# Early bias table, a reordered first step and a last tile stored as token rows in a one-core decoder layer

## The chip, the cores and the metric

The kernel runs on one core of one Trainium2 chip. The metric is the device time of one execution in microseconds (us). The engines are TensorE (PE in the profile, with PEld for its weight loads), VectorE (DVE), ScalarE (ACT), GpSimd (POOL) and SyncE (SP); each takes its instructions in the order in which the program lists them. SP, ACT and POOL also issue DMA transfers, which 16 DMA engines carry out; transfers issued by SP and ACT are the profile's hardware queues q1 and q10, those issued by POOL are its software queue q0.

## The reference

One step of a one-layer decoder with 1024 channels: 16 meta tokens and 2048 prompt tokens, and 8 sample tokens with caches. Cut to what matters here:

```python
def rmsnorm(x, g):
    return x * lax.rsqrt(jnp.mean(x * x, -1, keepdims=True) + 1e-6) * g

p = rmsnorm(x, norm1_g) @ w_in                  # 1024 -> 1792: q, k, v, GLU a, GLU b
u = p_a * sigmoid(p_b)
s = q @ k.T / 8 + rel_bias[t5_bucket(dist)]     # window 128, 8 heads, learned sinks
ao = softmax_with_sinks(s) @ v
cc = silu(layernorm(depthwise_conv31(u)))
x = x + concat(ao, cc) @ w_out                  # 1024 -> 1024
x = x + square(relu(rmsnorm(x, norm2_g) @ w_up)) @ w_down   # 1024 -> 4096 -> 1024
y = rmsnorm(x, norm_f_g)
```

The outputs are y for the prompt and for the samples, and the new key, value and convolution states. The change touches how the table `rel_bias[t5_bucket(dist)]` is laid out on the chip, the first matrix products, and how the last y leaves.

## The kernel before, in words

Channels lie on the partitions and tokens along the free dimension. The tokens are cut into five tiles of 384, 448, 448, 448 and 320 tokens; tile 0 carries the 16 meta tokens as well (400 columns), the last one the 8 samples (328 columns).

The weights come as 86 slabs of 128 x 1024 floats, used 424 times. One *step* (`pe_step`) multiplies one slab with one tile. Products keep fp32 accuracy by splitting each operand into two fp32r halves: the slab is loaded (`dma_slab`, SP, 512 KB), ACT casts it to `whi`, DVE subtracts for `wlo` (`split_slab`), and 24 products go into one PSUM buffer: for each of 8 chunks whi with the high and the low half of the activations, and then the 8 products with wlo. There are two `raw` buffers and three of each split half, so the load of slab k+2 waits for the `wlo` of slab k. PSUM: three buffers "mm" for steps, two "s" and two "pt" for attention (the fourth and fifth step of tile 0 borrow "pt"), one "st" for sums.

Slabs are counted here from 0, in the order in which they are loaded. The start is `norm1_first`: slab 0, the 8 chunks of tile 0, the split of h1 = x*g, and warm-up products. It does not wait for the row scale `rs` of the first norm; the step results are multiplied by `rs` when they leave PSUM (`ev0`). So the first result can leave only after `rs`, which takes 8 squares, sums on PE, a root, a reciprocal, a broadcast on PE and a copy on ACT (`rstd` with quick). Eight steps of tile 0 run like this, then tile 1 joins.

`bias_setup` builds the bias table for attention. A product on PE gives 8 heads x 384 values, ACT copies them to SBUF, POOL writes them to two tables in DRAM, `scr` (8 copies) and `skw` (16 copies, each a position further along), and 8 reads of `skw` (16 partitions each) fill `bias` with 128 x 8 x 256 values. Its reads wait until `skw` has landed. It is called ahead of the second step (nin == BAT). POOL also loads x of tile 1, ahead of it.

The end is `final_gen` for the last tile: squares on ACT, their sum over chunks on DVE, column sums on PE, root, reciprocal and broadcast, then 8 times y*g*rs on DVE, each stored as 128 x 328 by SP or ACT.

The Tile framework orders the instructions of each engine by a simulated time line and by priorities; a changed call place can therefore move others.

Of the kernel before, what the change touches and what calls it, by code (L numbers as in the profile page):

```python
# [7 lines left out]
F32 = mybir.dt.float32  # L8
F32R = mybir.dt.float32r
AF = mybir.ActivationFunctionType  # L10
ALU = mybir.AluOpType
PSUM = bass.MemoryType.PSUM

D = 1024
# [62 lines left out]
            self.step(DRAIN)  # L77


def trunk(tc, x_in, w_all, smalls, rel, ck, cv, sconv, y_out, kv_out, ck_out, cv_out, up_out, us_out):  # L80
    nc = tc.nc
    with ExitStack() as ctx:
        cp = ctx.enter_context(tc.tile_pool(name="cp", bufs=1))
# [130 lines left out]
        def pe_step(hi, lo, n, evac, budget, late=False, parts=1, keep=False, spare=False):  # L214
            k = cur[0]
            if not keep:
                cur[0] += 1
            while pos["split"] <= min(k + LA, len(order) - 1):
                split_slab()
            while pos["dma"] < min(k + LA + 1 + NRAW, len(order)):  # L220
                dma_slab()
            if late:
                flush()
            wh, wl = split[k] if keep else split.pop(k)
            if spare:
                ps = pa.tile([128, 512], F32, tag="pt", name="mm")
            else:
                ps = pm.tile([128, 512], F32, tag="mm", name="mm")
            o = ps[:, :n]
            seq = []  # L230
            if late:
                for c in range(8):
                    seq += [(wh, hi, c), (wh, lo, c), (wl, hi, c)]
            else:
                for c in range(8):
                    seq += [(wh, hi, c), (wh, lo, c)]
                seq += [(wl, hi, c) for c in range(8)]
            cut = [len(seq) * (p + 1) // parts for p in range(parts)]
            for j, (w, a, c) in enumerate(seq):
                mm(o, w[:, c, :], a[c], j == 0, j == len(seq) - 1)  # L240
                if j + 1 == cut[0]:
                    old = list(pend)
                    pend.clear()
                    for e in old:
                        e()
                if j + 1 in cut:
                    bg.step(budget / parts)
            pend.append(lambda: evac(ps))
# [116 lines left out]
        def norm1_first():  # L365
            s = st[0]
            n = TI[0]
            dma_slab()
            x = s["x"] = load_x(0)
            dma_slab()  # L370
            with tc.high_priority(2000):
                split_slab()
                warm = misc()
                for _ in range(WARM):
                    mm(warm[:, :128], ones, ones, True, True)
                s["h1h"], s["h1l"] = [], []
                for c in range(8):
                    hi = slot(F32R)
                    lo = slot(F32R)
                    act(hi[:, :n], x[c][:, :n], AF.Copy, scale=sm[:, G1 + c:G1 + c + 1])  # L380
                    stt(lo[:, :n], x[c][:, :n], sm[:, G1 + c:G1 + c + 1], f(hi[:, :n]), ALU.mult, ALU.subtract)
                    s["h1h"].append(hi)
                    s["h1l"].append(lo)
            split_slab()
            g1 = norm1_gen(1)
            next(g1)
            box = []
            s["rs"] = slot()
            for _ in ahead(run_stats(norm_stats(x, n, quick="a0" in QUICK, gate=s["h1h"][7], out=s["rs"]), box), 2000):
                pass  # L390
            return g1

# [515 lines left out]
        def down_step(i, g, d, budget):  # L908
# [10 lines left out]
                flush()  # L919
            pe_step([t[:, :n] for t in s["hh"]], [t[:, :n] for t in s["hl"]], n, ev, budget, late=d == 0)  # L920

        def final_gen(i):
            s = st[i]
            n = RT[i]
            s.setdefault("ydone", 0)
            box = []
            yield from run_stats(norm_stats(s["x2"], n, ready=lambda c: s["ydone"] > c,
                                             quick="f%d" % i in QUICK), box)
            rs = box[0]
            for c in range(8):  # L930
                y = s["x2"][c]
                stt(y[:, :n], y[:, :n], sm[:, GF + c:GF + c + 1], rs[:, :n], ALU.mult, ALU.mult)
                q = (nc.sync, nc.scalar)[c % 2] if i == NT - 1 else nc.gpsimd
                q.dma_start(y_out[:, YO[i] + c * n:YO[i] + (c + 1) * n], y[:, :n])  # L934
                yield

        def bias_setup():
            ps = misc()
            mm(ps[:NH, :EW], relt[:33, 0:NH], relt[:33, 8:8 + EW], True, True)
            e = slot()  # L940
            cpy(e[:NH, :EW], ps[:NH, :EW])
            nc.gpsimd.dma_start(scr.rearrange("p h x -> h p x"),
                                e[:NH, :EW].unsqueeze(1).broadcast_to([NH, NSMP, EW]))
            a = skw[:]
            row = NH * SKWW
            nc.gpsimd.dma_start(bass.AP(tensor=a.tensor, offset=a.offset, ap=[[SKWW, NH], [row + 1, NSKW], [1, EW]]),
                                e[:NH, :EW].unsqueeze(1).broadcast_to([NH, NSKW, EW]))
            for q in range(0, 128, NSKW):
                nc.gpsimd.dma_start(bias[q:q + NSKW], bass.AP(tensor=a.tensor, offset=a.offset + 127 - q,
                                                              ap=[[row, NSKW], [SKWW, NH], [1, 256]]))  # L950
# [80 lines left out]
        for op in prog:  # L1031
            k = op[0]
            if k == "in":
                _, i, m = op
                if i == 0:
                    if nin == N1AT:
                        gens["n1"] = [bg.add(g1)]
                    if nin == BAT:
                        bias_setup()
                    nin += 1  # L1040
                win_step(i, m, 24 * (TI[i] / 2400.0) - 1.2 - 0.6, spare=i == 0 and nin in (4, 5))
            elif k == "in2":
                m = op[1]
                win_step(0, m, 24 * (TI[0] / 2400.0) - 1.2 - 0.6, keep=True)
                win_step(1, m, 24 * (TI[1] / 2400.0) - 0.6)
            elif k == "conv0":
                flush()
                gens["conv"] = [bg.add(ahead(conv_gen(0), HP0, lambda: "ln" in st[0])), bg.add(conv_pe_gen(0), True)]
            elif k == "attn0":
                flush()  # L1050
                gens["attn"] = [bg.add(attn_gen(0, range(j, PT[0] // BQ[0], NS0)), A0F) for j in reversed(range(NS0))]
            elif k == "out":
                _, i, m = op
                wout_step(i, m, ff_budget(i, False))
            elif k == "ff":
                _, i, t, g, c = op
                b = ff_budget(i, t == "u")
                if t == "u":
                    up_step(i, g * 8 + c, b)
                else:  # L1060
                    down_step(i, g, c, b)
            elif k == "bg":
                i = op[1]
                flush()
                cat_alloc(i)
                gens["attn"] = [bg.add(attn_gen(i, range(j, PT[i] // BQ[i], NS1))) for j in range(NS1)]
                if i == NT - 1:
                    gens["attn"].append(bg.add(sample_gen(i)))
                gens["conv"] = [bg.add(ahead(conv_gen(i), HPC, lambda: "ln" in st[i]))]
            elif k == "sync_bg":  # L1070
                flush()
                bg.drain(gens["attn"] + gens["conv"])
            elif k == "n1":
                gens["n1"] = [bg.add(norm1_gen(op[1]))]
            elif k == "sync_n1":
                bg.drain(gens["n1"])
            elif k == "n2":
                gens["n2"] = [bg.add(ahead(norm2_gen(op[1]), HPN if op[1] else HPN0))]
            elif k == "sync_n2":
                flush()  # L1080
                bg.drain(gens["n2"])
            elif k == "fin":
                gens["fin"] = [bg.add(ahead(final_gen(op[1]), HPF if op[1] == NT - 1 else 0))]
                if op[1] == NT - 1:
                    flush()
                    bg.drain()
# [14 lines left out]
HPC = 0  # L1101
HPN = 0
HPN0 = 300
HPF = 0
COV = 5
BAT = 1
WARM = 12
N1AT = 3
A0F = True
QUICK = ["a0", "a1", "l0", "m0", "b0", "f4"]  # L1110
NS0 = 2
NS1 = 1
NPB = 2
# [6 lines left out]
def _pack(inp):  # L1120
# [62 lines left out]


_OUTS = [
    ("y_out", (128, 8 * sum(RT))), ("kv_out", (128, 2, 128 + NSMP)), ("ck_out", (128, 1024)),
    ("cv_out", (128, 1024)), ("up_out", (128, 4, CW - 1)), ("us_out", (128, 4, NSMP, CW)),
]

# [38 lines left out]
```

## Time and profile before

| | us |
|---|---|
| median of 3 runs | 2097.62 (2097.12 to 2098.48) |
| profiled execution, whole time | 2097.54 |
| its span, first to last instruction | 2095.7 |
| PE busy in the span | 2068.3 (99%) |
| DVE busy | 1525.2 (73%) |
| ACT busy | 1181.0 (56%) |
| mean granted TensorE clock | 0.993 of full |

The span is followed by 1.8 us that the profile does not show. A busy share is a mean over the whole span; the start (about 75 us) and the end (about 12 us) have other limits than the middle, and they are read from stretches of their own.

### The profile page before, as it was taken

What the parts mean: (1) busy time and instruction counts of PE and PEld (TensorE: products, weight loads), DVE (VectorE), ACT (ScalarE), POOL (GpSimd) and SP (SyncE); (2) the same over time, 40 slices, a digit from 0 to 9 for tenths busy, and PEclk for the clock granted to TensorE, in tenths of its full rate; (3) what the DMA queues carried; (4) which work ended last, traced back from release to release, by engine and by line L of the source; (5) the groups of instructions that cost most, each with busy time, mean ns of one, the idle gap of its engine ahead of it and who ended that gap; (6) DMA issues with size and microseconds to landing.
All of it is one profiled execution on the core that took longest, in us unless ns stands there. A gap on an engine that the chain in (4) does not pass through costs nothing.

```text
span 2095.7 us, 30054 instructions
## 1 busy us (share of the span) xinstructions
PE 2068.3 (99%) x11354; PEld 1961.5 (94%) x11354; DVE 1525.2 (73%) x2603; ACT 1181.0 (56%) x2154; POOL 55.8 (3%) x111
## 2 busy tenths in 40 slices
PE   9899999999999999999999999999999999999998
PEld 8688899999999999999999999999999999999997
DVE  7896798977858987658669886567797754564444
ACT  7577565667456456564454647555646465454443
POOL 3000000000000000000000000000011000000000
PEclk9899999999999999999999999999999999999999
DMA  7113233334532222234323222244433322444443
GB/s 209 47 37 111 100 122 104 128 114 160 179 111 101 101 101 101 101 136 162 129 104 108 101 101 101 101 172 150 142 117 112 123 105 101 151 162 151 151 143 105
DMA packets 77536, 254.39 MB, mean 121 GB/s; under 512 B 9661, under 2 KB 20037, under 8 KB 77392
## 3 DMA queue, kind: packets, MB, share of 16 engines
q1 hardware_dynamic: 72000, 238.08, 32.5%
q0 software_dynamic: 4672, 13.65, 2.3%
q8 instruction: 89, 1.46, 0.3%
q10 hardware_dynamic: 720, 0.76, 0.1%
q14 instruction: 55, 0.45, 0.1%
HBM read 241.97 MB, written 10.47 MB: 120 GB/s over the span
## 4 chain that ended last, share of the span: by engine, by line
PE 95%; DVE 2%; DMA 1%; ACT 1%; issue 0%; POOL 0%; SPq 0%; DVEq 0%; ACTq 0%; POOLq 0%
PE mm L159 89%; PE st L159 2%; PE pt L595 1%; PE s L159 1%; DVE t L119 1%; DMA bias<-skw 0%; DMA skw<-t 0%; DVE t L115 0%; PE cps L159 0%; DVE m L119 0%; ACT p L135 0%; DMA raw<-w_all 0%; DVE p L576 0%; DMA sm<-smalls 0%; ACT L134 0%
## 5 line engine op out<-in xcount | busy, mean ns | idle before, releaser
L159 PE MATMUL mm<-t,whi 128*128 128x448 f32 (+3 forms) x6560 | 1330.9, 349 | 3.1 <-ACT t L138 0.8
L159 PEld LDWEIGHTS mm<-t,whi 128*128 128x128 f32 x6560 | 1164.1, 188 | 58.2 <-DVE t L115 2.9
L138 ACT CAST whi<-raw 128x1024 fp32r<-128x1024 f32 x424 | 443.5, 1049 | 546.6 <-PE mm L159 430.2
L159 PE MATMUL mm<-t,wlo 128*128 128x448 f32 (+3 forms) x3280 | 702.6, 347 | 0.0
L115 DVE TENSOR_TENSOR wlo<-raw,whi 128x1024 fp32r<-128x1024 f32 x424 | 516.6, 1218 | 224.7 <-PE mm L159 123.5
L159 PEld LDWEIGHTS mm<-t,wlo 128*128 128x128 f32 x3280 | 587.9, 188 | 24.9
L119 DVE SCALAR_TENSOR_TENSOR t<-u,sm,t 128x448 f32<-128x448 f32 (+1 forms) x480 | 300.5, 645 | 3.5
L115 DVE TENSOR_TENSOR t<-mm,t 128x448 f32<-128x448 f32 (+2 forms) x200 | 116.5, 583 | 184.5 <-PE mm L159 181.4
L115 DVE TENSOR_TENSOR t<-m,t 128x448 fp32r<-128x448 f32 (+3 forms) x236 | 134.1, 581 | 25.8 <-ACT t L138 25.1
L138 ACT CAST t<-m 128x448 fp32r<-128x448 f32 (+3 forms) x236 | 125.3, 536 | 18.8 <-DVE m L119 14.6
L134 ACT ACTIVATE m<-mm 128x448 f32<-128x448 f32 (+2 forms) x176 | 90.2, 512 | 51.0 <-PE mm L159 49.5
L134 ACT ACTIVATE m<-t 128x448 f32<-128x448 f32 (+3 forms) x140 | 71.7, 542 | 61.7 <-DVE t L115 43.0
L134 ACT ACTIVATE m<-m 128x448 f32<-128x448 f32 (+3 forms) x164 | 90.1, 549 | 4.5 <-DVE m L115 0.6
L135 ACT ACTIVATE p<-p,nm 112x240 f32<-112x240 f32 (+3 forms) x152 | 72.3, 477 | 27.3 <-DVE nm L124 25.9
L576 DVE CUSTOM_DVE_ANT_0 p<-s,bias,sm 112x240 f32<-112x240 f32 (+3 forms) x152 | 61.1, 449 | 6.2 <-DMA bias<-skw 3.8
L134 ACT ACTIVATE p<-p,rd 112x240 f32<-112x240 f32 (+3 forms) x152 | 61.9, 476 | 3.9 <-DVE rd L130 3.5
L115 DVE TENSOR_TENSOR ss<-ss,m 128x448 f32<-128x448 f32 (+3 forms) x100 | 58.4, 584 | 6.3 <-ACT m L134 2.8
L934 POOL DMA_DIRECT2D y_out<-t x32 | 17.3, 543 | 1602.6 <-DVE t L119 1601.4
L130 DVE RECIPROCAL rs<-m 128x448 f32<-128x448 f32 (+2 forms) x15 | 41.6, 2776 | 23.9 <-ACT m L134 23.9
L119 DVE SCALAR_TENSOR_TENSOR t<-t,sm 128x384 f32<-128x384 f32 (+1 forms) x98 | 58.3, 612 | 0.9
L159 PE MATMUL mm<-cal,whi 128*128 128x448 f32 (+2 forms) x160 | 55.3, 347 | 0.2 <-DVE cal L115 0.2
L159 PE MATMUL mm<-cah,whi 128*128 128x448 f32 (+2 forms) x160 | 55.3, 347 | 0.0
(178 smaller groups left out, 1159.6 us busy)
## 6 DMA issues: line engine op xcount, KB each, us to landing
raw<-w_all SPq DMA_DIRECT2D x424, 512.0 KB, 3.2
t<-x_in SPq DMA_DIRECT2D x40, 224.0 KB, 4.6
y_out<-t POOLq DMA_DIRECT2D x24, 224.0 KB, 3.3
t<-x_in SPq DMA_DIRECT2D x16, 164.0 KB, 3.5
t<-x_in POOLq DMA_DIRECT2D x8, 224.0 KB, 4.3
t<-x_in SPq DMA_DIRECT2D x8, 200.0 KB, 4.6
t<-x_in SPq DMA_DIRECT2D x8, 192.0 KB, 3.8
y_out<-t POOLq DMA_DIRECT2D x8, 192.0 KB, 4.7
```

The source lines that it names most:

```text
L115: return nc.vector.tensor_tensor(out, a, b, op=op)
L119: return nc.vector.scalar_tensor_tensor(out, a, s, b, op0=op0, op1=op1)
L130: return nc.vector.reciprocal(out, a)
L134: return nc.scalar.activation(out, a, f, bias=bias, scale=scale)
L135: return nc.scalar.activation(out, a, f, bias=bias, scale=scale, accum_out=accum_out)
L138: return nc.scalar.copy(out, a)
L159: return nc.tensor.matmul(out, lhsT, rhs, start=start, stop=stop)
L576: nc.vector.tensor_tensor_reduce(out=p[:bq, c, :nk], in0=sp[c // 2][:bq, c % 2, :nk], in1=bias[:bq, h, b0:b0 + nk], scale=1.0, scalar=sm[: ...
L595: nc.tensor.transpose(t[:r, c * bq:(c + 1) * bq], p[:bq, c, a:a + r], idn[:bq, :bq])
L934: q.dma_start(y_out[:, YO[i] + c * n:YO[i] + (c + 1) * n], y[:, :n])
```

## The change

Three things are changed.

1. In the first step (`k == 0`) the 24 products are interleaved: chunk c with whi, then the two products of chunk c-1 that need `wlo` or the low half.
2. `bias_setup` is called in `norm1_first`, with a PSUM buffer of its own ("s"), and its POOL part is tied by a one-column copy to the eighth `h1h`. The gate of the squares moves from `h1h[7]` to `h1l[7]`.
3. The last tile ends in `final_last`: y*g is formed in place chunk by chunk, without rs. PE turns it (24 transposes, three windows of 110 tokens by 8 chunks of 128 channels) into six PSUM banks of 110 x 512; the sums of squares are taken per token, so that the scale is one value per partition; ACT and DVE scale the six banks into SBUF, and six stores of 109 or 110 rows x 512 floats (2 KB a row) go to a new output `yl_out`. The host no longer turns the last tile.

```diff
+            if k == 0:
+                for c in range(9):
+                    if c < 8:
+                        seq += [(wh, hi, c)]
+                    if c > 0:
+                        seq += [(wl, hi, c - 1), (wh, lo, c - 1)]
...
+                bias_setup(s["h1h"][7])
...
-            for _ in ahead(run_stats(norm_stats(x, n, quick="a0" in QUICK, gate=s["h1h"][7], out=s["rs"]), box), 2000):
+            for _ in ahead(run_stats(norm_stats(x, n, quick="a0" in QUICK, gate=s["h1l"][7], out=s["rs"]), box), 2000):
...
+        def final_last(i):
...
+            w = -(-n // 3)
+            at0 = [0, w - 1, n - w]
+            rows = [w - 1, n - 2 * w + 1, w]
...
+                if c == 7:
+                    yg.append(tmp())
+                    ts(yg[c][:, :n], y[:, :n], g, None, ALU.mult)
+                else:
+                    act(y[:, :n], y[:, :n], AF.Copy, scale=g)
...
+                for b in range(3):
+                    o = slice(at0[b], at0[b] + w)
+                    mm(ps[:w, b:b + 1], ssum[:, o], ones[:, 0:1], True, False)
+                    mm(ps[:w, b:b + 1], sqs[7][:, o], ones[:, 0:1], False, True)
+                act(r[:w, :3], ps[:w, :3], AF.Sqrt, bias=epst[:w], scale=1.0 / D)
+                recip(r[:w, :3], r[:w, :3])
+            for b in range(3):
+                nc.vector.tensor_copy(tb[b][1][:1, :1], sqs[7][:1, :1])
...
+                    if k % 2 == 0:
+                        act(o, tb[b][h][:w], AF.Copy, scale=r[:w, b:b + 1])
+                    else:
+                        ts(o, tb[b][h][:w], r[:w, b:b + 1], None, ALU.mult)
+                    q = nc.scalar if k == 4 else nc.sync
+                    q.dma_start(yl_out[at0[b]:at0[b] + rows[b], h * 512:h * 512 + 512], o[:rows[b]])
...
-                q = (nc.sync, nc.scalar)[c % 2] if i == NT - 1 else nc.gpsimd
-                q.dma_start(y_out[:, YO[i] + c * n:YO[i] + (c + 1) * n], y[:, :n])
+                nc.gpsimd.dma_start(y_out[:, YO[i] + c * n:YO[i] + (c + 1) * n], y[:, :n])
...
-        def bias_setup():
-            ps = misc()
+        def bias_setup(gate):
+            ps = pa.tile([128, 512], F32, tag="s", name="bs")
...
+            nc.gpsimd.tensor_copy(e[:NH, :1], f(gate[:NH, :1]))
...
-                    if nin == BAT:
-                        bias_setup()
...
-QUICK = ["a0", "a1", "l0", "m0", "b0", "f4"]
+QUICK = ["a0", "a1", "l0", "m0", "b0"]
```

What the order of the instructions makes of it is shown at three places.

POOL near the start, before: the loads of tile 1 (x_in), then the two tables, then the reads into the bias table. What a row waits for stands in brackets (DMASW: a POOL transfer, Activation: ACT).

```order
L355 DMA t<-x_in 128x448 [waits DMASW3_49,Pool_49]
L355 DMA t<-x_in 128x448 [waits DMASW4_49,Pool_49]
L942 DMA scr<-t 8x8x384 [waits DMASW5_49,Activation_49]
L946 DMA skw<-t 8x16x384 [waits DMASW6_49]
L634 DMA sbias<-scr 64x129 [waits DMASW7_49,DMASW5_49]
L949 DMA bias<-skw 16x8x256 [waits DMASW6_49,DMASW0_49]
```

The same place now:

```order
L361 DMA t<-x_in 128x448 [waits Pool_49]
L1017 DMA scr<-t 8x8x384 [waits Activation_49]
L1021 DMA skw<-t 8x16x384 [waits DMASW3_49]
L361 DMA t<-x_in 128x448 [waits DMASW4_49,Pool_49]
L361 DMA t<-x_in 128x448 [waits DMASW5_49,Pool_49]
L361 DMA t<-x_in 128x448 [waits DMASW6_49,Pool_49]
L641 DMA sbias<-scr 64x129 [waits DMASW7_49,DMASW2_49]
L1024 DMA bias<-skw 16x8x256 [waits DMASW3_49,DMASW0_49]
```

The two table writes stand ahead of the last three loads of tile 1, and what they wait for on ACT is a copy that now follows the cast of slab 1.

ACT around the copy of rs, before: `whi` are the casts of the slabs (449 is slab 5, 493 slab 6, 545 slab 7), rq and m the root and the broadcast operand, and the COPY from st is rs.

```order
L138 CAST whi_449<-raw_354 128x1024
L134 ACTIVATE rq_236<-st_231,epst_92 128x3
L134 ACTIVATE rq_236<-st_231,epst_92 16x1
L134 ACTIVATE m_242<-idn_85,rq_236 128x128 x3
L134 ACTIVATE m_242<-idn_85,rq_236 16x16
L138 CAST whi_493<-raw_399 128x1024
L138 COPY t_198<-st_241 128x400
L138 CAST whi_545<-raw_453 128x1024
```

The same place now (450 is slab 5, 494 slab 6, 546 slab 7):

```order
L138 CAST whi_450<-raw_355 128x1024
L134 ACTIVATE rq_251<-st_246,epst_92 128x3
L134 ACTIVATE rq_251<-st_246,epst_92 16x1
L134 ACTIVATE m_257<-idn_85,rq_251 128x128 x3
L134 ACTIVATE m_257<-idn_85,rq_251 16x16
L138 CAST whi_494<-raw_400 128x1024
L138 CAST whi_546<-raw_454 128x1024
L138 COPY t_213<-st_256 128x400
```

The copy of rs has moved behind the cast of slab 7.

PE at the end, before, from the last step on:

```order
L159 MATMUL mm<-t,whi 128x328 x16
L159 MATMUL mm<-t,wlo 128x328 x8
L159 MATMUL st<-ones,ss 128x1 x2
L159 MATMUL st<-ones,ss 72x1
L159 MATMUL st<-m,ones 128x128 x2
L159 MATMUL st<-m,ones 128x72
```

PE at the end now (yt are the transposes, m in the sums the squares of the last chunk):

```order
L159 MATMUL mm<-t,wlo 128x328 x8
L945 MATMUL yt<-idn,t 110x128 x8
L159 MATMUL st<-ones,ss 110x1
L945 MATMUL yt<-idn,t 110x128 x4
L159 MATMUL st<-ones,m 110x1
L159 MATMUL st<-ones,ss 110x1
L159 MATMUL st<-ones,m 110x1
L159 MATMUL st<-ones,ss 110x1
L159 MATMUL st<-ones,m 110x1
L945 MATMUL yt<-idn,t 110x128 x3
L945 MATMUL yt<-idn,m 110x128
```

Twelve transposes stand between the last step's products and the sums, twelve behind them (the last two rows repeat twice more). SP then issues five stores of 109, 109, 110, 109 and 110 rows, and ACT one of 109 rows.

## Rows read from the trace of the kernel before

**Rows 1.** The page: busy time and share of the span, by engine.
```profile
PE 2068.3 (99%) x11354; PEld 1961.5 (94%) x11354; DVE 1525.2 (73%) x2603; ACT 1181.0 (56%) x2154; POOL 55.8 (3%) x111
```

**Rows 2.** Timeline, PE: start, us, engine, line, instruction, idle before and releaser.
```profile
12.21 3.16 PE L159 MATMUL mm<-t,whi 128*128 128x400 f32 x16 [0.66 <-ACT whi L138]
15.20 1.60 PE L159 MATMUL mm<-t,wlo 128*128 128x400 f32 x8
```

**Rows 3.** Timeline, 30 to 33 us: rs, the first results, the cast of slab 7.
```profile
30.79 0.49 ACT L138 COPY t<-st 128x400 f32<-128x400 f32 x1 [1.44 <-PE st L159]
31.31 2.01 DVE L115 TENSOR_TENSOR m<-mm,t 128x400 f32<-128x400 f32 x4 [0.56 <-ACT t L138]
...
32.12 1.05 ACT L138 CAST whi<-raw 128x1024 fp32r<-128x1024 f32 x1 [0.84 <-PE mm L159]
```

**Rows 4.** The chain that ended last, 36 to 57 us: start, us, what.
```profile
36.30 7.75 DMA skw<-t
...
44.65 3.70 POOL bias L949 x7
48.35 7.81 DMA bias<-skw
```

**Rows 5.** Timeline, 56 to 69 us: attention's wait, and the begin of tile 1.
```profile
56.34 0.37 DVE L576 CUSTOM_DVE_ANT_0 p<-s,bias,sm 128x144 f32<-128x144 f32 x1 [3.82 <-DMA bias<-skw]
...
67.31 1.28 DVE L119 SCALAR_TENSOR_TENSOR m<-t,sm,rs 128x448 f32<-128x448 f32 x2 [0.24 <-ACT rs L138]
```

**Rows 6.** Stretches: bounds, length, busy (instructions) of PE, PEld, DVE, ACT, POOL, PEclk, DMA share, GB/s.
```profile
41.00:42.00 1.00, 1.00 (x8) 1.00 (x6) 1.00 (x3) 0.97 (x3) 0.00 (x0) 1.00 0.48 50
...
52.00:53.00 1.00, 0.18 (x1) 0.00 (x0) 0.51 (x1) 0.75 (x1) 0.00 (x0) 1.00 1.07 127
...
60.00:74.00 14.00, 10.38 (x36) 9.32 (x37) 13.39 (x29) 5.57 (x15) 0.00 (x0) 0.50 0.00 0
```

**Rows 7.** The only queue with data, 18:19.4 and 50.5:53: packets, MB, share of 16 engines.
```profile
q0 software_dynamic: 150, 0.55, 100.4%
...
q0 software_dynamic: 112, 0.31, 105.5%
```

**Rows 8.** The same, 9 to 11 us, while SP's transfers run.
```profile
q1 hardware_dynamic: 211, 0.77, 99.1%
```

**Rows 9.** Slab loads: one issue, and issue to landing in 25:30 and 47:52.
```profile
49.33 0.33 SPq L187 DMA_DIRECT2D raw<-w_all  x1
...
raw<-w_all SPq DMA_DIRECT2D x1, 512.0 KB, 3.0
...
raw<-w_all SPq DMA_DIRECT2D x1, 512.0 KB, 7.9
```

**Rows 10.** Timeline: ACT's cast of slab 4, POOL's last loads of tile 1.
```profile
22.10 1.05 ACT L138 CAST whi<-raw 128x1024 fp32r<-128x1024 f32 x1 [3.26 <-DMA raw<-w_all]
...
14.70 2.13 POOL L355 DMA_DIRECT2D t<-x_in  x4
```

**Rows 11.** The chain that ended last, in the tail.
```profile
2084.38 0.48 ACT m L134
...
2085.44 0.75 PE st L159 x6
...
2086.22 0.27 ACT rq L134
...
2086.51 0.18 DVE rq L130
```

**Rows 12.** Timeline of the tail: SP's stores.
```profile
2089.23 3.16 SPq L934 DMA_DIRECT2D y_out<-t  x4
```

**Rows 13.** DMA, 2080 to 2096 us: GB/s in 40 slices of 0.4 us.
```profile
GB/s 0 0 0 0 0 0 0 0 0 0 0 0 0 0 0 0 0 0 0 0 0 0 0 0 0 276 322 358 367 364 358 338 374 351 253 0 0 0 0 0
```

**Rows 14.** Groups of 90 to 130 us: attention's transposes, 128x512 casts out of PSUM.
```profile
L595 PE MATMUL pt<-idn,p 128*128 128x128 f32 x16 | 3.0, 272 | 0.0
...
L138 ACT CAST ph<-pt 128x512 fp32r<-128x512 f32 x4 | 2.3, 577 | 2.3 <-PE pt L595 2.3
```

More of the change, by code (lines that the diff above doesn't have):

```diff
@@ L77, in drain, with trunk @@
             self.step(DRAIN)
-def trunk(tc, x_in, w_all, smalls, rel, ck, cv, sconv, y_out, kv_out, ck_out, cv_out, up_out, us_out):
+def trunk(tc, x_in, w_all, smalls, rel, ck, cv, sconv, y_out, yl_out, kv_out, ck_out, cv_out, up_out, us_out):
     nc = tc.nc
@@ L230, in pe_step @@
             seq = []
-            if late:
+            if k == 0:
[4 more added lines that the diff above has]
+                        seq += [(wl, hi, c - 1), (wh, lo, c - 1)]
+            elif late:
                 for c in range(8):
@@ L920, in down_step, with turn @@
             pe_step([t[:, :n] for t in s["hh"]], [t[:, :n] for t in s["hl"]], n, ev, budget, late=d == 0)
+        def final_last(i):
+            s = st[i]
+            n = RT[i]
+            s.setdefault("ydone", 0)
+            w = -(-n // 3)
+            at0 = [0, w - 1, n - w]
+            rows = [w - 1, n - 2 * w + 1, w]
+            tb = [[pa.tile([128, 512], F32, tag="pt", name="yt"), pa.tile([128, 512], F32, tag="s", name="yt")],
+                  [pa.tile([128, 512], F32, tag="pt", name="yt"), pm.tile([128, 512], F32, tag="mm", name="yt")],
+                  [pa.tile([128, 512], F32, tag="s", name="yt"), pm.tile([128, 512], F32, tag="mm", name="yt")]]
+            ssum = tm.tile([128, TM], F32, tag="ss", name="ss", bufs=2)
+            sqs = []
+            yg = []
+            def turn(c):
+                for b in range(3):
+                    nc.tensor.transpose(tb[b][c // 4][:w, c % 4 * 128:c % 4 * 128 + 128], yg[c][:, at0[b]:at0[b] + w],
+                                        idn)
+            for c in range(8):
+                while s["ydone"] <= c:
+                    yield STEP
+                y = s["x2"][c]
+                g = sm[:, GF + c:GF + c + 1]
+                sq = tmp()
+                with tc.high_priority(400 if c == 7 else 0):
+                    act(sq[:, :n], y[:, :n], AF.Square)
+                sqs.append(sq)
+                if c == 7:
[3 more added lines that the diff above has]
+                    act(y[:, :n], y[:, :n], AF.Copy, scale=g)
+                    yg.append(y)
+                if c == 1:
+                    tt(ssum[:, :n], sqs[0][:, :n], sq[:, :n], ALU.add)
+                elif 1 < c < 7:
+                    tt(ssum[:, :n], ssum[:, :n], sq[:, :n], ALU.add)
+                if c < 4:
+                    turn(c)
+                yield
+            r = at.tile([128, 4], F32, tag="rq", name="rq", bufs=2)
+            with tc.high_priority(400):
+                ps = misc()
+                for b in range(3):
[4 more added lines that the diff above has]
+                recip(r[:w, :3], r[:w, :3])
+            for b in range(3):
+                nc.vector.tensor_copy(tb[b][1][:1, :1], sqs[7][:1, :1])
+            for c in range(4, 8):
+                turn(c)
+            bl = bias.rearrange("p h x -> p (h x)")
+            pl = at.tile([128, 4, 256], F32, tag="p", name="p", bufs=NPB).rearrange("p h x -> p (h x)")
+            k = 0
+            for h in range(2):
+                for b in range(3):
+                    o = bl[:w, k * 512:k * 512 + 512] if k < 4 else pl[:w, (k - 4) * 512:(k - 4) * 512 + 512]
+                    if k % 2 == 0:
[4 more added lines that the diff above has]
+                    q.dma_start(yl_out[at0[b]:at0[b] + rows[b], h * 512:h * 512 + 512], o[:rows[b]])
+                    k += 1
@@ L1082, in trunk @@
             elif k == "fin":
-                gens["fin"] = [bg.add(ahead(final_gen(op[1]), HPF if op[1] == NT - 1 else 0))]
+                gens["fin"] = [bg.add((final_last if op[1] == NT - 1 else final_gen)(op[1]))]
                 if op[1] == NT - 1:
@@ L1103 @@
 HPN0 = 300
-HPF = 0
 COV = 5
-BAT = 1
 WARM = 12
@@ L1185 @@
 _OUTS = [
-    ("y_out", (128, 8 * sum(RT))), ("kv_out", (128, 2, 128 + NSMP)), ("ck_out", (128, 1024)),
+    ("y_out", (128, 8 * sum(RT[:-1]))), ("yl_out", (RT[-1], D)), ("kv_out", (128, 2, 128 + NSMP)), ("ck_out", (128, 1024)),
     ("cv_out", (128, 1024)), ("up_out", (128, 4, CW - 1)), ("us_out", (128, 4, NSMP, CW)),
@@ L1210 @@
     y = r["y_out"]
-    yt = [y[:, YO[i]:YO[i] + 8 * RT[i]].reshape(128, 8, RT[i]).transpose(2, 1, 0).reshape(RT[i], D) for i in range(NT)]
-    yt = np.concatenate(yt, 0)
+    yt = [y[:, YO[i]:YO[i] + 8 * RT[i]].reshape(128, 8, RT[i]).transpose(2, 1, 0).reshape(RT[i], D) for i in range(NT - 1)]
+    yt = np.concatenate(yt + [r["yl_out"]], 0)
     y_prompt = np.ascontiguousarray(yt[None, :SEQ])
```

## The prediction, made before the changed kernel was run

> **What bounds the kernel now.** The busy row comes first: PE works 99% of the span [rows 1], so in the middle only fewer or faster products would save time, and the change makes none there. PE's slack lies at the start and in the tail, and both are touched; so I read these two stretches by timeline, chain of waits, stretches and DMA queues. At the start PE runs its steps from 12.21 [rows 2], but no result leaves PSUM before rs, copied at 30.79; the first evacuation follows at 31.31 [rows 3]. From there to tile 1 at 67.31 [rows 5] it is DVE's list that counts: 36.0 us, of which 3.82 are a wait for the bias table [rows 5]. That table is a DMA chain: the write of skw takes 7.75, then come the reads [rows 4]. In the tail the last product ends at 2083.76, the first store is issued at 2089.23 [rows 12], data flow from about 2090.0 to 2094.0 [rows 13], and the span ends 1.7 later, at 2095.7.
>
> **The first step.** It gets the same 24 products in another order. PE waits 0.66 for slab 1 before 12.21 and does the eight wlo products of step 0 only at 15.20 (8 of 0.18, 1.45 in all) [rows 2]. The new order puts them into step 0's waits for operands. The gain is between 0 (an operand later than its turn) and 1.45; it reaches the end only if rs or the casts follow PE. I take it as an earlier PE in the rival without collisions, and as nothing in the forecast, where slabs come late.
>
> **The bias table, earlier.** Its product moves into the warm-up and its ACT copy of about 0.4 behind the cast of slab 1, where ACT waits 3.26 for slab 4 later on [rows 10]; both cost nothing, at most 0.4 if that cover were gone. The copy on POOL costs one more short instruction. What counts are the DMAs. POOL finishes its last four loads' issues at 16.8 [rows 10]; now scr and skw are issued ahead of three of them, at about 16, and the eight reads as soon as skw has landed, about 25, instead of 44.65 [rows 4].
>
> What these transfers cost others is seen in two views. The tables' 0.295 MB go at 50 GB/s, with 0.48 of the 16 engines busy [rows 6]: 5.9 us, on half of the engines. The reads' 1.05 MB go at 127 GB/s on all engines [rows 6]: 8.3 us. And where POOL's packets are queued first, SP's do not get in between: with a slab issued at 49.33, the stretch from 50.5 to 53 holds packets of q0 only, at over 100% [rows 7, 9], and a slab that needs 3.0 in a quiet stretch needed 7.9 there [rows 9]. In the kernel before this hits slabs that have time. Now it hits slabs 4 to 7.
>
> The sum, for the engines that carry skw, if they are never idle: all of tile 1's loads were through at 19.4 [rows 7]; the last three (0.69 MB at 391 GB/s, from 0.77 MB at 99.1% in 2 us [rows 8]) are 1.8 of it, so the first five end at 17.6. Then 5.9 (tables), 1.8 (three loads), 4 slabs of 1.34 = 5.4, and 8.3 (reads): 39.0. Slab 7 lands then, if the reads go ahead of it. ACT's order now has the copy of rs behind the cast of slab 7: 1.05 + 0.49 and 0.1 of gaps give the first evacuation at 40.6 instead of 31.31, 9.3 later. DVE's list behind it holds the same work; the 3.82 of waiting for the table falls away, since the reads land by about 40. Net **+5.5**. [...]
>
> [...]
>
> **The last tile.** Work on PE, ACT and DVE beside the last steps is hidden: ACT (56% busy [rows 1]) takes seven more scalings. After the last product (2083.76): 12 transposes at 0.19 (3.0 / 16 [rows 14]) = 2.3, the first sum 0.25, five more at 0.125 (0.75 / 6 [rows 11]) = 0.6; the last chunk's evacuation and its square (ended by 2084.86, 0.48 [rows 11]) run beside them. Root 0.27 and reciprocal 0.18 [rows 11] with 0.05 of gaps: 2087.4. The first scaled bank of 512 columns takes 0.58 [rows 14]: the first store is issued at 2088.0, **1.2 earlier** than before [rows 12], and its data flow from 2088.8.
>
> Then the stores. Their bytes are the same 1.34 MB, in rows of 2 KB. Everything hangs on how many DMA engines carry 109 rows. Every transfer by SP or ACT in the trace has 128 rows and goes over all 16 engines. The tables have 8 rows outermost and used half of the engines, although each row holds many runs that could be spread [rows 6]; the reads have 16 and used all [rows 6]. So the cut goes along the outermost count and leaves engines idle rather than cutting finer. If it is into equal whole shares, 110 rows go to 11 engines (10 each), and 109, a prime, to one. If it is into shares as equal as possible, 109 go over 16. No row separates the two; I find equal shares likelier, since no transfer here has unequal ones.
>
> By equal shares, with the same engine first each time, one engine moves 4 x 109 + 2 x 10 = 456 rows = 933,888 bytes. One engine's rate is 24.3 GB/s with slab rows (0.77 MB / 2 us / 16 / 0.991 [rows 8]) and 21.9 to 23.4 with 1.3 KB rows (351 to 374 GB/s / 16 [rows 13]). For 2 KB rows I take 24.0: 38.9 us (38.4 to 42.6). Data end at 2127.7, the span at 2129.4: **+33.7**. By all engines it is 1.34 MB at 360 GB/s = 3.7, and the last bank is ready before 2090: end about 2094.5, **-1.2**.
>
> [...]
>
> **The rivals.**
> A, the forecast: one engine, late front: 2097.5 + 33.7 + 5.5 = 2136.7.
> B: one engine, but slabs get between POOL's packets. Then PE, 1.45 ahead, frees slab 4's buffer for the cast of slab 7 at 30.7 instead of 32.12 [rows 3]; the copy of rs ends at 32.3 at the latest, at most 1 later than before, and 3.8 of waiting go: about -3.2. 2097.5 + 33.7 - 3.2 = 2128.0. For it: four slabs and the reads may interleave in time even if they queue first-come. Against it: [rows 7].
> C: all engines, late front: 2097.5 - 1.2 + 5.5 = 2101.8.
> D, faster: all engines carry 109 rows and slabs are not held up: 2097.5 - 1.2 - 3.2 = 2093.1. It decides from the point where both the cut is unequal and slab 7 lands before 30.7.
> E: equal shares, but each store starts on another engine. The last of them, begun at about 2090.8, takes 109 x 2 KB at 24 GB/s = 9.3, and ends the span at 2102: +6.3, with the late front 2109.3.
> That the change does not do what it says: the table may be early and attention still wait, which is A's front with 1.4 to 3.8 more, inside the range.
>
> **How the numbers follow.** The profiled execution took 2097.54, the median 2097.62; so the sums stand for the median too. A 0.62, B 0.20, C 0.07, D 0.05, E 0.06. Equal shares from one engine thus have 0.82, my reading of the cut in [rows 6]; of the late front, three in four, by [rows 7]. The predicted time is A's, 2136.7. The range takes in A and B with their bounds: from B with the fast engine rate and a bit less of front (2125) to A with 42.6 us of stores and half a clock loss more (2144). Within 0.2% (2093.4 to 2101.8, about what a measurement of this kernel tells from no change) lies half of C. Faster 0.05, same 0.04, slower 0.91.
>
> **What would show it.** In the profile of the changed kernel: a tail of some 45 us behind the last product with DMA at about 24 GB/s, a sixteenth share (A, B); or stores over by 2095 (C, D). At the start: slabs 4 to 7 landing 5 to 10 us after issue, and the first evacuation near 40 (A, C), or near 32 (B, D); no wait for bias in attention. I am wrong outright if SP's 109 rows use all 16 engines.

## The result, and the profile after

The changed kernel took 2143.89 us, the median of 4 runs (2142.78 to 2145.40), the kernel before 2097.73: a ratio of 1.022, 95% interval 1.0203 to 1.0238. The forecast was 2136.7, the range 2125 to 2144; the time lies 0.1 inside the range's upper edge, and two of the four runs (2144.98 and 2145.40) lie above it. The profiled execution took 2142.78, its span is 2140.7.

Two differences carry the whole loss. First, how late each slab is. The table is worked out from the timelines: the start of the wlo subtraction of a slab in the changed kernel less that in the kernel before.

```
slab                    3     4     5     6     7    10    13    16    17    21 ... 420
later by, us         1.22  4.76  8.67 12.26 10.88 13.08  9.91 13.38 16.15 12.82 ... 13.24
```

All the delay has arisen by slab 22 (208 us); from there to the tail it stays at 13.2. ACT's timeline at the start shows where it begins (start, us, engine, line, instruction, idle before and releaser):

```profile
26.86 1.04 ACT L138 CAST whi<-raw 128x1024 fp32r<-128x1024 f32 x1 [6.79 <-DMA raw<-w_all]
33.41 1.04 ACT L138 CAST whi<-raw 128x1024 fp32r<-128x1024 f32 x1 [5.50 <-DMA raw<-w_all]
...
40.56 1.04 ACT L138 CAST whi<-raw 128x1024 fp32r<-128x1024 f32 x1 [3.55 <-DMA raw<-w_all]
42.48 1.04 ACT L138 CAST whi<-raw 128x1024 fp32r<-128x1024 f32 x1 [0.88 <-DMA raw<-w_all]
43.44 0.49 ACT L138 COPY t<-st 128x400 f32<-128x400 f32 x1
```

These are slabs 4 to 7 and the copy of rs. In the kernel before slab 4 was cast at 22.10 [rows 10] and slab 7 at 32.12, with rs copied at 30.79 [rows 3]. Each cast now ends a wait for a slab's DMA. On POOL's timeline the tables are written at 16.01 and the reads into bias begin at 25.09 (44.65 before [rows 4]):

```profile
16.01 0.64 POOL L1017 DMA_DIRECT2D scr<-t  x1
16.64 0.63 POOL L1021 DMA_DIRECT2D skw<-t  x1
...
25.09 2.15 POOL L1024 DMA_DIRECT2D bias<-skw  x4 [2.58 <-DMA skw<-t]
27.92 0.53 POOL L1024 DMA_DIRECT2D bias<-skw  x1 [0.68 <-DMA t<-x_in]
30.25 0.53 POOL L1024 DMA_DIRECT2D bias<-skw  x1 [1.80 <-DMA t<-x_in]
33.32 1.05 POOL L1024 DMA_DIRECT2D bias<-skw  x2 [2.53 <-DMA t<-x_in]
```

DVE's timeline gives the rest: the first evacuation at 43.95 (31.31 before [rows 3]), a wait for PE, and tile 1 at 78.03 (67.31 before [rows 5]). Attention no longer waits for bias.

```profile
43.95 0.57 DVE L115 TENSOR_TENSOR m<-mm,t 128x400 f32<-128x400 f32 x1 [0.94 <-ACT t L138]
...
51.69 1.23 DVE L115 TENSOR_TENSOR wlo<-raw,whi 128x1024 fp32r<-128x1024 f32 x1 [2.44 <-PE mm L159]
...
78.03 1.28 DVE L119 SCALAR_TENSOR_TENSOR m<-t,sm,rs 128x448 f32<-128x448 f32 x2 [0.24 <-ACT rs L138]
```

The second difference is the tail. Its timeline has the end of the last product on PE, and SP and ACT issuing the stores:

```profile
2095.62 1.36 PE L159 MATMUL mm<-t,wlo 128*128 128x328 f32 x8
...
2100.58 21.07 SPq L994 DMA_DIRECT2D yl_out<-bias  x4
...
2101.74 0.51 ACTq L994 DMA_DIRECT2D yl_out<-p  x1
2121.69 8.75 SPq L994 DMA_DIRECT2D yl_out<-p  x1
```

And stretches of it (columns as in rows 6: bounds, length, five engines, PEclk, DMA share, GB/s), with the two queues in 2110 to 2118, and the one that is left in 2124 to 2130 (packets, MB, share of 16 engines):

```profile
2101.40:2105.40 4.00, 0.00 (x0) 0.00 (x0) 0.61 (x1) 0.31 (x1) 0.00 (x0) 0.91 0.06 15
2104.00:2110.00 6.00, 0.00 (x0) 0.00 (x0) 0.00 (x0) 0.00 (x0) 0.00 (x0) 0.56 0.06 25
2110.00:2120.00 10.00, 0.00 (x0) 0.00 (x0) 0.00 (x0) 0.00 (x0) 0.00 (x0) 0.50 0.07 26
2124.00:2130.00 6.00, 0.00 (x0) 0.00 (x0) 0.00 (x0) 0.00 (x0) 0.00 (x0) 0.50 0.07 26
2130.90:2131.60 0.70, 0.00 (x0) 0.00 (x0) 0.00 (x0) 0.00 (x0) 0.00 (x0) 0.50 0.66 164
```
```profile
q1 hardware_dynamic: 51, 0.10, 3.3%
q10 hardware_dynamic: 50, 0.10, 3.3%
...
q1 hardware_dynamic: 77, 0.15, 6.6%
```

Two queues together keep 6.6% of 16 engines busy, which is one engine, at 26 GB/s; when SP's queue is left alone, it keeps the same 6.6% busy at the same rate, so both used one engine. The last stretch is a store of 110 rows: it keeps 0.66 of the engines busy, near 11 of 16. Before, the same bytes went at up to 374 GB/s [rows 13]. The last product ends at 2096.99, so 43.7 us of the span lie behind it, against 11.9 before.

### The profile page after: what moved, and what is told of

It is laid out like the page before. It is cut to its first block, busy times and chain, and to the rows that moved or that the text cites. A ratio compares the mean times of both kernels' runs of the same rounds, so it can differ in the third digit from the quotient of the medians.

```text
span 2140.7 us, 30104 instructions
## 1 busy us (share of the span) xinstructions
PE 2074.9 (97%) x11378; PEld 1968.5 (92%) x11378; DVE 1522.8 (71%) x2600; ACT 1185.2 (55%) x2159; POOL 56.2 (3%) x112
## 4 chain that ended last, share of the span: by engine, by line
PE 93%; DVE 3%; DMA 1%; ACT 1%; issue 0%; DVEq 0%; ACTq 0%
PE mm L159 87%; PE st L159 2%; PE s L159 1%; DMA raw<-w_all 1%; PE pt L602 1%; DVE t L119 1%; DVE t L115 0%; DVE wlo L115 0%; PE cps L159 0%; ACT p L135 0%; DVE m L119 0%; ACT whi L138 0%; DVE p L583 0%; DVE ss L115 0%; ACT p L134 0%
```

## The experiments

Beside each group of experiments the kernel before ran on the same chip; its medians there were 2097.58 (e1 to e4), 2097.27 (e5 to e8), 2097.53 (e9 to e11) and 2097.29 (e12).

**e1: other row counts in the changed kernel.**

```diff
-            w = -(-n // 3)
-            at0 = [0, w - 1, n - w]
-            rows = [w - 1, n - 2 * w + 1, w]
+            w = 112
+            at0 = [0, w, n - w]
+            rows = [w, w, n - 2 * w]
...
-                    q.dma_start(yl_out[at0[b]:at0[b] + rows[b], h * 512:h * 512 + 512], o[:rows[b]])
+                    q.dma_start(yl_out[w * b:w * b + rows[b], h * 512:h * 512 + 512], o[w - rows[b]:])
```

> The changed kernel with one difference: the three windows of the last tile give stores of 112, 112 and 104 rows instead of 109, 109 and 110. Theory (a store of 109 rows from SP or ACT is carried by one DMA engine): 112 and 104 divide among 16 and 13 engines, the stores are over in some 4 us instead of 38, and the span behind the last product shrinks from 43.7 to about 11 us: about 2109.6 us, which is the kernel before (2097.5) less 1.2 in the tail plus 13.2 from the start. Rival (rows of 2 KB, or the new tail as a whole, are slow whatever the count): no change, above 2140.

Measured: 2109.83 (2103.82 to 2112.40), ratio 1.0052 (1.0035 to 1.0069). The rival falls. Its DMA view of 2080 to 2102 (GB/s in 40 slices):

```profile
GB/s 0 0 0 0 0 0 0 0 0 0 0 0 0 0 0 0 0 0 0 0 0 0 0 0 0 0 52 272 294 238 205 257 253 291 242 279 60 0 0 0
```

The same bytes, in the same rows of 2 KB, at 205 to 294 GB/s instead of 26. The kernels with the changed start vary from run to run, and the profiled run of e1 is its fastest, so what is said below of e1's loss in microseconds is rough.

**e2: the changed start with the old tail** (`final_gen` for every tile, "f4" in QUICK, y_out as before).

> The changed first step and the early bias table, with the tail of the kernel before. Theory (the 13.24 us by which every slab runs late in the changed kernel arise in the first 180 us and have nothing to do with the last tile): 2097.7 + 13.2 = 2110.9 us. Rival (the new tail's instructions cost time beside the last steps too): below 2107.

Measured: 2111.75 (2108.75 to 2113.84), 14.2 above the kernel before. The rival falls; the start alone carries its loss.

**e3: the new tail alone, 112 rows** (first step, `bias_setup` and its place as before).

> The kernel before with only the new last tile, in stores of 112, 112 and 104 rows. Theory: the tail by itself gains 1.2 us once all engines carry it: 2096.5 us. Rival (the new tail is slow whatever the row count): about 2130. A third way (it gains nothing, since the six banks are ready later than the eight old results): 2097.7 or a little above.

Measured: 2096.37 (2095.91 to 2097.06), ratio 0.9994 (0.9984 to 1.0003): 1.2 below in the medians, as forecast, though the interval includes no change. In the profile the tail has only 0.5 of it: the last product ends at 2083.08 and the span at 2094.5, so 11.4 us lie between them against 11.9 before. The rest is a last product that ended 0.7 earlier, in steps that this kernel shares with the kernel before.

```profile
2081.72 1.36 PE L159 MATMUL mm<-t,wlo 128*128 128x328 f32 x8
...
2086.69 1.70 SPq L987 DMA_DIRECT2D yl_out<-bias  x4
```

**e4: the table held until rs.**

```diff
+            e = slot()
+            nc.gpsimd.tensor_copy(e[:NH, :1], gate)
+            nc.gpsimd.tensor_copy(e[:NH, :EW], e0[:NH, :EW])
             nc.gpsimd.dma_start(scr.rearrange("p h x -> h p x"),
```

(e0 is the table's copy, gate is rs; product and ACT copy stay early.)

> As e1_rows112, but POOL's table writes wait for rs (about 31 us) instead of the eighth h1h, so that no table transfer stands ahead of slabs 4 to 7; POOL copies the 8 x 384 table once more. Product and ACT copy of the table stay early, the interleaved first step stays, and so does the copy of rs behind the cast of slab 7. Theory (the start is lost to table transfers ahead of the slabs): first evacuation near 32, a short wait for bias or none, 2093.5 to 2095.5 us. Rival (the new order of the casts and of the first step loses the time): the same as e1_rows112, about 2109.6.

Measured: 2096.37 (2095.46 to 2098.88), 13.5 below e1. The rival falls: with the interleaved first step and the copy of rs behind the cast of slab 7 still there, the loss of the start is gone once the table's transfers stand behind slabs 4 to 7. It was 1 to 3 us above what I expected, since rs came later and POOL's two copies took 1.7 us, so attention still waited 1.6 for bias.

**e5: the table right behind rs on ACT.** The kernel before with the 112-row tail, the table's product in the PSUM buffer that the change gave it, and in place of the call at the second step:

```diff
             for _ in ahead(run_stats(norm_stats(x, n, quick="a0" in QUICK, gate=s["h1h"][7], out=s["rs"]), box), 2000):
                 pass
+            with tc.high_priority(2000):
+                bias_setup()
             return g1
```

> The kernel before with the new tail in 112, 112 and 104 rows, its own first step, and the bias table called right behind the statistics: ACT copies the table to SBUF directly behind rs (about 31.3) and ahead of the cast of slab 7, so that POOL can write the tables at about 32 instead of 35.7. Theory (the tables only hurt when they are queued ahead of slabs 4 to 7, and attention's wait of 3.8 us shrinks by what they are earlier): a wait of 0.1 to 0.5, 2096.4 - 3.4 = 2093.0 us. Rival (now they delay slabs 8 and 9 instead, and the wait moves there): 2096 or more.

Measured: 2094.54 (2093.92 to 2095.80), ratio 0.9986 (0.9976 to 0.9995), faster than both kernels. ACT's timeline has the two copies behind each other, and then the cast of slab 7:

```profile
31.21 0.49 ACT L138 COPY t<-st 128x400 f32<-128x400 f32 x1 [1.54 <-PE st L159]
31.60 0.46 ACT L138 COPY t<-bs 8x384 f32<-8x384 f32 x1
32.54 1.05 ACT L138 CAST whi<-raw 128x1024 fp32r<-128x1024 f32 x1 [0.48 <-ACT t L138]
```

The wait for bias is gone, as the theory says, but only 1.8 of the 3.4 us came. A part of the rest is the rival's: DVE now waits 1.03 for the cast of slab 10, whose load was issued at 47.36, while the reads were under way, and was waited for until 50.82. The other 0.6 I did not trace.

**e6: tables early, reads late.** As e1, but POOL's eight reads wait for rs.

> As e1_rows112, but the eight reads into the bias table wait for rs on POOL; the two table writes stay where the change put them, ahead of three loads of tile 1. Theory (the writes cost slabs 4 and 5 some 4 us, the reads the rest): slab 4 lands near 26, first evacuation at 34 to 36, 2096 to 2100 us. Rival (the writes, on half of the engines, do the harm by themselves): as e1_rows112, 2109.8.

Measured: 2103.90 (2101.19 to 2104.72). Neither was right: the reads account for some 5.9 of e1's loss (e1's fastest run lies inside the range of e6), the early writes for the larger part: e6 is still 7.4 above e10 (below), which has the same first step and no early writes, and 7.5 above e4, which has the table's product and copy early too. Slab 4 was cast at 26.26, as expected, but slab 7 at 35.45 and rs was copied at 36.41.

**e7: a third raw buffer.** As e1 with `NRAW = 3`.

> As e1_rows112 with three raw slab buffers instead of two. Theory (a late slab also delays the issue of the second one behind it, because its buffer is free only after its wlo; that is why the start lost 13 us where the queueing sum gave 5.5): the loads of slabs 4 to 7 are issued 4 to 8 us earlier and 4 to 8 of the 13 us come back: 2102 to 2106 us. Rival (it is queueing alone): 2109.8.

Measured: 2100.43 (2096.56 to 2103.44), 9.4 below e1. The rival falls; the gain is larger than I allowed.

**e9: its control.** As e5 with `NRAW = 3`.

> As e5_table_behind_rs with three raw buffers: the control for e7_three_raw. Theory (in e7 the third buffer gave back 9.4 us because it loosened the issue of slabs that were held up by the table's transfers): here, where no slab up to 7 is held up, it is worth the wait for slab 10 alone (DVE waits 1.0 for its cast near 51.9 in e5): 2093.0 to 2094.5 us. Rival (a third buffer helps this kernel wherever): 2085 to 2090.

Measured: 2097.71 (2095.71 to 2099.33), 3.2 above e5: neither was right, and where no slab is held up early, the third buffer does not help. Its loss does not arise at the start: up to slab 13 its wlo run as early as in e5 (2.5 against 2.2 ahead of the kernel before), though DVE waits 1.9 for bias, and at slab 22 they are 1.1 behind the kernel before, e5's still 2.2 ahead. What costs 3.6 between these two slabs I did not follow up. So the third buffer by itself is no gain, and what e7 got back goes with the slabs that are held up.

**e8: 110 rows.** As e3, in stores of 110, 110 and 108 rows.

> As e3_tail112_only, but in stores of 110, 110 and 108 rows. Theory (as many engines as the largest number up to 16 that divides the rows: 11, 11 and 12): the data take about 1.4 times as long as over 16 engines, 1 to 2 us more than e3_tail112_only, about 2097.5 us. Rival (every count that 16 does not divide goes to one engine): 1.34 MB at 26 GB/s = 51 us, above 2140. Second rival (109 was slow for another reason than its divisors, and 110 shares it): about 2129.

Measured: 2097.51 (2096.83 to 2097.90), 1.1 above e3. Both rivals fall: one row more than 109, and 30 us are gone. While its data flowed, from 2086.7 to 2092.4, 0.5 to 0.8 of the engines were busy in slices of 0.3 us; in 2088 to 2091 of e3 two queues held 95.5% of them. Behind its last product lie 12.6 us, 1.2 more than in e3.

**e10: the interleaved first step**, with the squares tied to h1l[7] as in the change, added to e5.

> As e5_table_behind_rs with the interleaved first step (and the squares tied to h1l[7], as in the change). Theory (PE gains up to 1.45 us at the start, but the order then puts the copy of rs behind the cast of slab 7, and everything that counts follows rs): first evacuation 0.5 to 2 us later than the 31.74 of e5, 2095 to 2096.5 us. Rival (PE's lead counts): 2093 to 2094.

Measured: 2096.55 (2095.54 to 2097.34), 2.0 above e5. ACT's timeline shows what the order turned round:

```profile
29.62 1.05 ACT L138 CAST whi<-raw 128x1024 fp32r<-128x1024 f32 x1 [2.84 <-DMA raw<-w_all]
30.57 1.18 ACT L134 ACTIVATE m<-idn,rq 128x128 f32<-128x128 f32 x4
32.34 1.04 ACT L138 CAST whi<-raw 128x1024 fp32r<-128x1024 f32 x1 [0.59 <-DMA raw<-w_all]
33.29 0.48 ACT L138 COPY t<-st 128x400 f32<-128x400 f32 x1
```

rs is copied 2.1 later than in e5, behind the cast of slab 7. That is one turn; the other is that m, the operand of rs's broadcast, is made at 30.57, behind the cast of slab 6, where e5 makes it at 27.55, ahead of it. DVE then does the wlo of slab 7 first, and the first evacuation comes at 34.71, 3.0 later than in e5 and not 0.5 to 2. The changed kernel has the turn at slab 7 alone, so the 2.0 are the price of e10's order and not of its own.

**e11: the tail alone with 109 rows** (as e3, rows as in the change).

> The kernel before with the new tail as the change has it, 109, 109 and 110 rows: the price of the one engine without the start. Theory (start and tail add up: 2143.9 is 2097.5 + 13.2 + 33): 2097.5 + 32 to 33 = 2129.5 to 2130.5 us. Rival (they do not add up): outside 2127 to 2133.

Measured: 2127.88 in one run, 30.4 above the kernel before and 31.5 above e3. With the 14.2 of e2, 2097.6 + 30.4 + 14.2 = 2142.2, against 2143.89 measured: the two parts add up, within the few us by which kernels with the changed start vary from run to run.

```profile
2080.97 1.36 PE L159 MATMUL mm<-t,wlo 128*128 128x328 f32 x8
```

Its span ends at 2126.1, 43.8 behind this last product, as in the changed kernel (43.7). So the tail costs the same 31.8 in both. That the run lies 1.6 below my 2129.5 comes from the last product, which ended at 2082.3, 1.4 earlier than in the kernel before.

**e12: contiguous stores.** As e5, output as (2, 328, 512).

> As e5_table_behind_rs, with the output of the last tile laid out as two halves of 328 x 512, so that each store writes one contiguous piece instead of 2 KB pieces 4 KB apart. In e3 and e5 the stores over 16 engines moved about 250 GB/s, the 1.3 KB rows of the kernel before about 350. Theory (the pieces 4 KB apart slow the writes): 1.34 MB at 350 GB/s instead of 250 saves 1.5 us, 2093.0 us. Rival (the row length of 2 KB with 112 rows, or the 13 engines of 104 rows, sets the rate): as e5, 2094.5.

Measured: 2094.51 (2093.93 to 2095.57), as e5. In 2087.5 to 2091 the stores of both moved the same: first e12, then e5.

```profile
DMA packets 473, 0.85 MB, mean 243 GB/s; under 512 B 58, under 2 KB 58, under 8 KB 473
```
```profile
DMA packets 480, 0.86 MB, mean 247 GB/s; under 512 B 58, under 2 KB 58, under 8 KB 480
```

The 4 KB distance of the pieces is not what keeps these stores below the 350 GB/s of the kernel before. Nor is it mainly idle engines: in this stretch of e5 two queues hold 68.7% and 21.6% of the 16 engines, 90% together. What does stays open.

## Why the prediction came out as it did

**The stores of 109 rows: right, a little too dear.** Forecast +33.7, measured +31.8 in the spans of the changed kernel and of e11 (43.7 - 11.9). The step that no row separated from its rival, equal whole shares, held here: 109 rows went to one engine (6.6% of 16 busy), and 110 rows kept 0.66 of them busy and cost 1.1 us more than 112 (e8). The 6.6%, for two queues at once and for one of them alone, says that both queues used the same engine, as the sum took it. The 1.9 are made of small terms: the first store was issued 3.6 behind the last product and not 4.2, data flowed for 38.1 us (2101.4 to 2139.4) and not 38.9, and the span ended 1.3 behind them and not 1.7. That the data term came so close is partly luck: the engine moved 26 GB/s and not 24.0, by which 933,888 bytes take 35.9, but only 15 in the first 4 us, which the sum did not hold. Rival E (another engine for each store) and C and D (all engines) are out.

**The tail without that: right in its sum, by luck in its terms.** The first store was issued 3.6 us behind the last product's end (2100.58 - 2096.99), against 5.5 before: 1.9 earlier, forecast 1.2. But the stores over all engines went at some 250 GB/s, where I had put 360: from the first issue to the end of the span e3 takes 7.8 us, the kernel before 6.5. So 1.3 of the 1.9 are lost again, and of the 1.2 that e3 gained the tail has 0.5.

**The start: right in kind, wrong in size.** Forecast +5.5; measured +14.2 (e2), +13.24 in the profiled run. Its parts, against the sum:

- The landing of slab 7. The sum said 39.0, "if they are never idle". It was cast at 42.48, behind a wait for its DMA. The engines did fall idle: between 38 and 42 the DMA share is 0.49 (below), and slab 7 had been issued only at 35.74, because its buffer came free with the wlo of slab 5, itself cast at 33.41. I had named the two raw buffers, and the wait of slab k+2 for slab k, among the facts, and then made a sum of bytes that did not hold it. e7 with e9 shows that this link matters: a third buffer takes off 9.4 where slabs are held up and gains nothing where they are not.
- The first evacuation: 43.95 against 40.6, 3.4 later, all of it from the landing.
- The clock. After a wait of 4.26 PE ran at 0.50 of full clock in both stretches below, and DVE, whose list I had taken as unchanged, waited 2.44 for it at 51.69. From the first evacuation to tile 1 it took 34.1 instead of 32.2. The sum of +5.5 held nothing of this; the range allows for half a clock loss, which was my estimate and which no run shows as a term by itself; what the runs showed in its place is the 0.50 and these 1.9 us. PE's wait, and the stretches:

```profile
36.28 2.18 PE L159 MATMUL st<-m,ones 128*128 128x128 f32 x8 [4.26 <-ACT m L134]
...
38.00:42.00 4.00, 1.76 (x5) 1.19 (x5) 0.36 (x1) 1.04 (x1) 0.00 (x0) 0.50 0.49 114
46.00:48.00 2.00, 2.00 (x7) 1.97 (x7) 2.00 (x5) 0.00 (x0) 0.00 (x0) 0.50 0.60 199
```

- Later: tile 1 began 10.7 late, from slab 22 on they are 13.2 late. The growth begins at slab 13 (9.9 late, at 112 us) and has reached 13.4 at slab 16 (151 us). Between 166 and 176 PE was busy for 7.51 of 10 us at a mean clock of 0.84, where it had run at 1.00 before, but by then the 13.4 were there. e2 and e6, with tables early too, grow in the same way (8.0 to 12.7 and 3.2 to 6.6). What makes the delay grow I have not tested. The sum held nothing of it.

**First come, first served: only half right.** I argued from [rows 7] that SP's packets do not get between POOL's. The changed kernel has stretches of both kinds. Slab 4's load was issued at 17.45 (in the kernel before, where nothing else was under way, a load issued at 24.44 moved data from 25.4 on). In 18.5 to 20 us POOL's queue is all but alone at work, and in 31 to 33 both queues share the engines:

```profile
q0 software_dynamic: 175, 0.51, 121.2%
q1 hardware_dynamic: 2, 0.00, 1.1%
```
```profile
q0 software_dynamic: 56, 0.15, 55.3%
q1 hardware_dynamic: 49, 0.18, 54.3%
```

The reads were not queued in one go either: POOL waited for loads of tile 1 between them (27.92, 30.25, 33.32 in its timeline above), so slabs came between. Why the first stretch has POOL's queue all but alone and the second both was not shown. The sharing did not bring rival B's time: the load of slab 6, issued at 29.19, shared the engines with the reads and took 11.3 to land, against 3.0 in a quiet stretch [rows 9].

**The first step's order: the step of the sum held; what the order costs by itself is not shown.** PE did come 1.4 ahead (step 2 begins at 16.88 instead of 18.27), and it was worth nothing here. The sum of A held the order as the 1.05 us of a cast ahead of rs, and rival B let it cost at most 1. Where slabs are on time, the interleaved first step cost 2.0 (e10), but with a second turn on ACT that the changed kernel does not have.

**The wait for bias: right.** The 3.82 are gone.

Over all, the tail was 1.9 too dear and the start 7.7 too cheap (5.5 against 13.24): 2136.7 - 1.9 + 7.7 = 2142.5, against 2142.78 of the profiled execution. The step that failed is the start's sum of bytes: it left out the chain from a late slab to the issue of the second one behind it (3.4 us), held nothing of the slow clock (1.9) and knew nothing of the later growth (2.5), whose cause stays open. The time is right within the range because the larger term was right; that it is still inside, by 0.1, is luck, since the two errors partly cancel.

## What to carry to other kernels

Look at the number of rows of every store before its bytes: 109 rows of 2 KB went through one DMA engine at 26 GB/s, stores of 112, 112 and 104 rows over many at some 250, and this cut of 328 instead of 109, 109 and 110 was worth 31.5 us (e11 against e3) to 34.1 (the changed kernel against e1). The table's transfers, moved ahead of slabs 4 to 7, cost 13.5 us (e1 against e4): put what is moved early behind the loads that the path is waiting for, and where loads have few buffers (a third was worth 9.4 us in e7, where loads were late, and nothing in e9), follow one late load to the issue of the next before adding up bytes. And look at what a scheduler turned round on the engine that holds the one value everyone waits for: one cast ahead of rs's broadcast and one ahead of rs went with a loss of 2.0 us (e10).

## What the runs showed of the hardware that I had not expected

One engine alone moved 2 KB rows at 26 GB/s, with 6.6% of the 16 busy. Sixteen together moved 293 GB/s in the first 1.2 us of e5's 112-row stores, with all of them busy, which is 18 each:

```profile
2086.20:2087.40 1.20, 0.00 (x0) 0.00 (x0) 0.44 (x1) 0.15 (x1) 0.00 (x0) 1.00 1.01 293
```

The 1.3 KB rows of the kernel before went at some 350; contiguous targets made no difference (2094.51 in e12, 2094.54 in e5). While one engine worked through the 109-row stores, SP's third store took 18.16 us to issue (SP's timeline of the changed kernel):

```profile
2102.83 18.16 SPq L994 DMA_DIRECT2D yl_out<-bias  x1
```

So this issue was held for 18.16 us while stores were under way. No run here tells what limits either.
